# A hybrid convolution and attention layer on one core: the causal zero block kept in its tiles, sixteen modulation dots beside the attention heads, gate products in twos, and a paired last quarter

## The chip, the cores and the metric

The kernel runs on one core of one Trainium2 chip. The metric is the device time of one execution in microseconds (us), the median of several runs. Each engine (PE, the matrix engine; DVE, the vector engine; ACT, the scalar engine; POOL; SP, which here only issues transfers) takes its own list of instructions in a fixed order, and semaphores hold an instruction back until what it needs is there.

## What is computed

One layer: a modulation vector from the condition `c`, then a mixing sub-layer that runs a causal convolution and stick-breaking attention on the same modulated input and merges them by two gates, and then a SwiGLU sub-layer. Width 1024, 1024 rows, 8 heads of 64, 31 taps, all in float32. Cut to what matters:

```python
mod = silu(c) @ ada_w + ada_b                        # 6 x 1024
sh1, sc1, ga1, sh2, sc2, ga2 = split(mod, 6)
h = rmsnorm(x, pre_mix_g) * (1 + sc1) + sh1
proj = h @ w_in                                      # glu_in, qkv, gates
u = u_val * sigmoid(u_gate)
y_conv = silu(layernorm(causal_depthwise_conv(u))) @ w_conv_out
# stick-breaking attention, causal is strict: s_idx < t_idx
log_keep = where(causal, log_sigmoid(-z), 0)
a = where(causal, exp(log_sigmoid(z) + cumsum_reverse(log_keep) - log_keep), 0)
y_att = (a @ v) @ w_att_out
y = (sigmoid(g_conv) * y_conv + sigmoid(g_att) * y_att) @ w_o
x = x + ga1 * rmsnorm(y, post_mix_g)
h = rmsnorm(x, pre_ffn_g) * (1 + sc2) + sh2
x = x + ga2 * rmsnorm((silu(gate) * up) @ w_ffn_out, post_ffn_g)
```

## The kernel before

Every float32 operand is split into a high and a low part (`hi` and `lo`), and a product is three matmuls; ACT makes the high part and DVE the low one. The stages stand one after the other on PE: norms and first projections to about 70 us; the attention stage from 70 to about 430 us; the early gate products to 500; the rest of the gate products (`other_five`) with the layer norm (`ln_all`) to 560; `y_conv`, `y_att` and the output projection to 760; the SwiGLU products to about 1185; its output sweeps to 1403, and the finish of the last quarter of the output.

In the attention stage `attend(p)` treats head pair p. A head takes blocks of 256 query rows, c = 0 to 3. For each it makes the logits `z` (PE, L551 to L554), two sigmoids (`ka` and `be`, ACT), a scan of products and a multiply (DVE, L559 and L561), and then for each pair of key blocks `jp` four 128 x 128 transposes into one PSUM tile `tr` (PE, L571), a copy to `ahi` (ACT, L574), a subtraction to `alo` (DVE, L575) and four `av` matmuls with the values `vst` (L580, L581). In the diagonal pair (jp == c) one of the four blocks lies behind the causal bound, and a tile `zeros` is transposed for it. Between the heads' instructions stand the gated units `glu(ct)` (products `pgg` and `pgv`, result `u`, stored to `v_d`), `conv(ct)` (`pcv` matmuls, results `co` stored to `u_d`), the value products `v_half` (`pv`, split into `vst` at L485 and L486) and the next pair's `pq` and `pk`. A scheduler of the language sets the order on each engine from the order of the code, from priorities and from its own estimates.

`load` issues a transfer on SP's queue and `store` on POOL's; a queue takes its instructions in order, and one that waits holds up those behind it. A tile with a `tag` and `bufs=1` shares one buffer with all tiles of that tag: the next user waits until the last one is done.

`dot_c` is one column of the modulation vector: a multiply by the condition and a sum along the row on DVE (L135, 128 x 1024). Columns 16 to 31 (`ada2_16` to `ada2_31`), first needed after the output projection, stand between the `y_conv` tiles, two behind each, loaded on SP into two buffers. The last quarter of the output is finished by `finish(..., last=...)`: a root (L151 to L155), two multiplies with it (L1637, L1640) and the add of the residual (`add`, L1540).

## Time and profile before

| | us |
|---|---|
| median of 3 runs (1415.29 to 1421.37) | 1417.07 |
| the profiled execution | 1416.81 |
| span of the profiled execution | 1415.0 |
| PE busy in the span | 1383.6 (98%) |
| DVE busy | 1060.4 (75%) |
| ACT busy | 651.3 (46%) |

The profile is of one execution; its span is the time between the first and the last instruction that it records, and the rest of the device time lies around it. An engine is busy while one of its instructions runs. Matmuls overlap, so that the duration of a single one is longer than the distance to the next. Names are those of the program without buffer numbers, and L12 is line 12 of the kernel.

### The profile page before, as it was taken

To read this page: it belongs to the slowest core of one execution; us is meant where nothing else is said; L and a number is where in the kernel's file an instruction comes from. 1 tells how busy PE (TensorE), PEld (TensorE's weight loads), DVE (VectorE), ACT (ScalarE), POOL (GpSimd) and SP (SyncE) were. 2 spreads that over 40 slices of the span, in tenths; PEclk is the share of its full clock that TensorE was granted. 3 is DMA by queue.
4 is the path that set the end of the run, shared out by engine and by line. 5 is a ranking of instruction groups with operands and counts; after the bars stand their busy time and mean duration, and the time that the engine had idled before them with its cause. 6 is when DMAs were issued, how large, how long until landed. Compare 5 with 4: busy or idle time off the path is not lost.

```text
span 1415.0 us, 18809 instructions
## 1 busy us (share of the span) xinstructions
PE 1383.6 (98%) x6886; PEld 1156.1 (82%) x6886; DVE 1060.4 (75%) x1602; ACT 651.3 (46%) x1136; POOL 96.7 (7%) x183
## 2 busy tenths in 40 slices
PE   7999999999999999999999999999999999999996
PEld 4798898898888878888877778888888887888886
DVE  6898598576767789779588878778877775775357
ACT  5375465364553447412356553334444453334441
POOL 0000000000001110000012100001111110000000
PEclk8999999999999999999999999999999999999998
DMA  9112041131253645784935545456777769588833
GB/s 382 74 37 75 30 141 54 45 114 66 77 177 111 228 179 175 280 277 137 361 120 173 185 147 173 157 173 228 242 255 246 259 245 392 170 333 280 281 116 119
DMA packets 91116, 258.73 MB, mean 183 GB/s; under 512 B 9744, under 2 KB 20112, under 8 KB 90000
## 3 DMA queue, kind: packets, MB, share of 16 engines
q1 hardware_dynamic: 75088, 202.99, 42.1%
q0 software_dynamic: 15936, 54.54, 10.3%
q8 instruction: 54, 0.88, 0.3%
q14 instruction: 38, 0.31, 0.1%
HBM read 190.91 MB, written 66.58 MB: 182 GB/s over the span
## 4 chain that ended last, share of the span: by engine, by line
PE 80%; DVE 6%; issue 6%; DMA 5%; ACT 2%; POOL 1%; SPq 0%; DVEq 0%; POOLq 0%; ACTq 0%
PE ka L958 12%; PE ka L1500 8%; PE kc L958 7%; PE pwo L881 6%; PE pb L1500 4%; PE pgv L180 3%; PE pg L180 3%; PE pyc L180 3%; PE pya L180 3%; PE pv L481 3%; PE pcv L461 3%; PE tr L571 2%; PE pq L180 2%; PE pgg L180 2%; PE pk L180 2%
## 5 line engine op out<-in xcount | busy, mean ns | idle before, releaser
L559 DVE TENSOR_TENSOR_SCAN ka<-ka 128x128 f32<-128x128 f32 (+2 forms) x96 | 91.4, 968 | 22.8 <-ACT ka L555 22.5
L555 ACT ACTIVATE ka<-z 128x128 f32<-128x128 f32 (+2 forms) x96 | 47.1, 496 | 58.8 <-PE z L554 34.4
L575 DVE TENSOR_TENSOR alo<-tr,ahi 128x512 fp32r<-128x512 f32 x80 | 53.2, 685 | 18.2 <-ACT ahi L574 17.5
L1500 PE MATMUL ka<-gt,w2f 128*128 128x512 f32 x264 | 63.4, 390 | 0.8 <-DMA w2f<-w_d 0.8
L574 ACT ACTIVATE ahi<-tr 128x512 fp32r<-128x512 f32 x80 | 46.3, 601 | 38.1 <-PE tr L571 25.8
L561 DVE TENSOR_TENSOR be<-be,ka 128x127 f32<-128x127 f32 (+2 forms) x96 | 53.4, 573 | 9.6 <-ACT be L556 4.9
L1500 PEld LDWEIGHTS ka<-gt,w2f 128*128 128x128 f32 x264 | 49.4, 188 | 11.5 <-issue 1.4
L1066 PE MATMUL ke<-b,w_hi 128*128 128x512 f32 x176 | 55.2, 394 | 0.0
L135 DVE SCALAR_TENSOR_TENSOR ada<-ada,cb 128x1024 f32<-128x1024 f32 x32 | 38.8, 1223 | 20.7 <-DMA ada<-in_ada_dram 20.6
L556 ACT ACTIVATE be<-z 128x128 f32<-128x128 f32 (+2 forms) x96 | 46.2, 495 | 9.5 <-PE tr L571 9.3
L571 PE MATMUL tr<-ident,be 128*128 128x128 f32 x288 | 47.8, 273 | 0.4 <-DVE alo L575 0.4
L580 PE MATMUL av<-ahi,vst 128*128 128x256 f32 x160 | 44.2, 292 | 0.0
L461 PE MATMUL pcv<-ph,cvw 128*128 128x128 f32 x320 | 42.5, 276 | 0.8 <-DMA ph<-v_d 0.8
L581 PE MATMUL av<-alo,vst 128*128 128x256 f32 x160 | 42.8, 293 | 0.0
L461 PEld LDWEIGHTS pcv<-ph,cvw 128*128 128x128 f32 x320 | 39.5, 192 | 1.5 <-issue 1.2
L1066 PEld LDWEIGHTS ke<-b,w_hi 128*128 128x128 f32 x176 | 33.0, 188 | 7.8 <-issue 1.0
L481 PE MATMUL pv<-wv_hi,hhi 128*128 128x256 f32 x128 | 36.8, 288 | 2.1 <-DVE qst L505 1.4
L159 ACT ACTIVATE gt<-X 128x512 fp32r<-128x512 f32 x33 | 20.4, 630 | 39.5 <-DVE X L1543 12.4
L481 PE MATMUL pv<-wv_hi,hlo 128*128 128x256 f32 x128 | 36.7, 287 | 0.0
L481 PE MATMUL pv<-wv_lo,hhi 128*128 128x256 f32 x128 | 36.4, 285 | 0.0
L551 PE MATMUL z<-kst,qst 128*128 128x256 f32 (+2 forms) x96 | 36.2, 382 | 0.0
L571 PEld LDWEIGHTS tr<-ident,be 128*128 128x128 f32 x288 | 34.7, 140 | 1.8 <-PE z L554 0.5
(533 smaller groups left out, 4097.7 us busy)
## 6 DMA issues: line engine op xcount, KB each, us to landing
w_d<-w2o POOLq DMA_DIRECT2D x44, 512.0 KB, 8.0
w2f<-w_d SPq DMA_DIRECT2D x44, 512.0 KB, 5.4
ada<-in_ada_dram SPq DMA_DIRECT2D x32, 512.0 KB, 6.1
w2r<-in_w_dram SPq DMA_DIRECT2D x44, 256.0 KB, 3.8
w1g<-in_w_dram SPq DMA_DIRECT2D x21, 512.0 KB, 3.6
w1u<-in_w_dram SPq DMA_DIRECT2D x21, 512.0 KB, 5.2
cvw<-in_cvw_dram SPq DMA_DIRECT2D x20, 512.0 KB, 3.7
ada_w<-in_ada_dram SPq DMA_DIRECT2D x8, 1024.0 KB, 12.0
```

The source lines that it names most:

```text
L180: pe.matmul(bank, st[:, cols], mv[k][:, c * CH:(c + 1) * CH], start=(i == 0 and s == 0), stop=(i == n - 1 and s == 2))
L461: pe.matmul(cv[:, gi * TM:(gi + 1) * TM], wts[n][:, at:at + P], ph[:, g, SH - 1 - d:SH - 1 - d + TM], start=(d == 0), stop=(d == SH - 1))
L481: pe.matmul(pv[:, :256], st[k][:, tcols], mv[:, wc], start=(k == 0 and i == 0), stop=(k == KT - 1 and i == 2))
L555: act.activation(kap[:, s_lo:s_hi], z[:, zo:zo + w], AF.Sigmoid, bias=0.0, scale=-0.125)
L559: dve.tensor_tensor_scan(rev, rev, rev, init, op0=ALU.mult, op1=ALU.bypass)
L561: dve.tensor_tensor(beta[:, :m], beta[:, :m], kap[:, s_lo + 1:s_lo + 1 + m], op=ALU.mult)
L571: pe.transpose(tr[:, o:o + P], src, ident)
L575: dve.tensor_tensor(alo, tr, ahi, op=ALU.subtract)
L881: pe.matmul(bank_, st[:, cols], mv[k][:, cs], start=(k == 0 and q == 0), stop=(k == KT - 1 and q == 2))
L958: pe.matmul(bank_, st[:, cols], t[:, mv], start=(first and j == 0 and s == 0), stop=(j == HK - 1 and s == 2), skip_group_check=not first)
L1066: pe.matmul(kbs[f], wes[f][st][:, cols], t[:, mv], start=(i == 0 and j == 0 and q == 0), stop=(j == HK - 1 and q == 2), skip_group_check=i ...
L1500: pe.matmul(dst, w[st][:, cols], g[mv], start=first and s == 0, stop=last and s == 2, skip_group_check=more)
```

## The change

Seven edits. (1) The transposes of `zeros` are gone. The diagonal pair goes to one of two lasting pairs of tiles, `diag_t`, whose first 128 columns are set to zero once; the two key blocks of that pair change places in the tile, and the copy and the subtraction cover 384 columns instead of 512. (2) The sixteen dots move from `y_conv` into the attention stage: six behind `glu(0)`, five behind `glu(1)`, five behind `glu(2)`. They are loaded on POOL's queue into the one buffer of tag `u`, which `glu` also uses. The small operations behind the dots (`add_bias`, `fold_gate`) move with them in the order on DVE. (3) The stores of `co` move from SP's to POOL's queue. (4) `conv(3)` moves behind the first plain gate. (5) The early gate products run two gates at a time, and the second product of each is added in the bank of the first: six adds on DVE (L628) are gone. (6) The last tile of `y_att` is finished in two halves with a higher priority, and the rotation of banks is shifted by one. (7) The last quarter's finish copies three residual pieces into PSUM on ACT, does the first of four output pieces on POOL, and adds in 512 columns instead of 256 on DVE.

```diff
@@ conv
-                    load(u_d[ct][hf * (NG // 2):(hf + 1) * (NG // 2)].rearrange("g p m -> p g m"), o)
+                    store(u_d[ct][hf * (NG // 2):(hf + 1) * (NG // 2)].rearrange("g p m -> p g m"), o)
@@ head
+            diag_t = []
+            for i in range(2):
+                t = [pa.tile([P, CH], F32R, name=f"{nm}d{i}") for nm in ("ahi", "alo")]
+                for x in t:
+                    dve.tensor_copy(x[:, :P], zeros)
+                diag_t.append(t)
+            ndiag = count()
...
+                            on = jp == c
                             for jj in range(2):
                                 j = 2 * jp + jj
                                 for ii in range(2):
+                                    if on and jj == 1 and ii == 0:
+                                        continue
                                     jo = (j - 4 * sc) * P
-                                    src = zeros if (jp == c and jj == 1 and ii == 0) else probs[ii][:, jo:jo + P]
-                                    o = jj * 256 + ii * P
-                                    pe.transpose(tr[:, o:o + P], src, ident)
-                            ahi = pa.tile([P, CH], F32R, tag="ahi", name=f"ahi{tag}_{c}_{jp}", bufs=2)
-                            alo = pa.tile([P, CH], F32R, tag="alo", name=f"alo{tag}_{c}_{jp}", bufs=2)
-                            act.activation(ahi, tr, AF.Copy)
-                            dve.tensor_tensor(alo, tr, ahi, op=ALU.subtract)
+                                    o = (jj ^ on) * 256 + ii * P
+                                    pe.transpose(tr[:, o:o + P], probs[ii][:, jo:jo + P], ident)
+                            if on:
+                                ahi, alo = diag_t[next(ndiag) % 2]
+                                used = slice(P, CH)
+                            else:
+                                ahi = pa.tile([P, CH], F32R, tag="ahi", name=f"ahi{tag}_{c}_{jp}", bufs=2)
+                                alo = pa.tile([P, CH], F32R, tag="alo", name=f"alo{tag}_{c}_{jp}", bufs=2)
+                                used = slice(0, CH)
+                            act.activation(ahi[:, used], tr[:, used], AF.Copy)
+                            dve.tensor_tensor(alo[:, used], tr[:, used], ahi[:, used], op=ALU.subtract)
...
-                                cols = slice(jj * 256, jj * 256 + 256)
+                                cols = slice((jj ^ on) * 256, (jj ^ on) * 256 + 256)
@@ the attention stage
+            a2 = deque(range(2 * KT, 4 * KT))
+
+            def ada2_dots(n):
+                for _ in range(n):
+                    col = a2.popleft()
+                    w = pc.tile([P, D], F32, tag="u", name=f"ada2_{col}", bufs=1)
+                    store(w, ada2[col - 2 * KT])
+                    dot_c(w, cb, col)
+
             for p in range(4):
                 glu(p)
+                ada2_dots((6, 5, 5, 0)[p])
                 if p == 2:
                     v = v_half(1)
                 if p:
                     conv(p - 1)
                 qk = attend(p, qk, v)
-            conv(3)
             for n in PLAIN:
+                if n == PLAIN[1]:
+                    conv(3)
...
-            for i in GPAIRS:
...
-                k2 = bank(f"k2_{i}")
-                prod0(k2, w_op(f"a12_{i}", raw[:, CH:], act, dve), "B21")
-                dve.tensor_tensor(e[1], k2, e[0], op=ALU.add)
-                act.activation(e[1], e[1], AF.Sigmoid, bias=0.0, scale=1.0)
+            for i0 in range(0, len(GPAIRS), 2):
+                two = GPAIRS[i0:i0 + 2]
...
+                for i in two:
+                    prod0(ek[i], a12[i], "B21", False)
+                    e1 = sgp.tile([P, CH], F32, tag="sg", name=f"ee1_{i}", bufs=2)
+                    act.activation(e1, ek[i], AF.Sigmoid, bias=0.0, scale=1.0)
+                    store(s_d[2 * i][:, :CH], e1)
@@ y_conv and y_att
-            ada2_dots(y_conv(n), 2)
+            y_conv(n)
...
+        next(uidg)
...
+            if n == KT - 1:
+                hi, lo = (hp.tile([P, T], F32R, tag="act", name=f"{nm}{n}") for nm in ("mhi", "mlo"))
+                for c in range(NCH):
+                    gemm({c: yb[c]}, wa, (ohi, olo), range(4), woff=(n % 2) * CH)
+                with tc.high_priority(offset=LASTM):
...
@@ finish
+            if last:
+                xp = {}
+                for mm_ in (2, 3, 1):
+                    xp[mm_] = bank(f"x1p{mm_}").rearrange("p (a b) -> p a b", a=2)
+                    act.activation(xp[mm_], xrs[c, mm_][:, :, cols], AF.Copy)
             rstd_from(rs, m, a, ps_sum, D)
+            if last:
...
+                pool.tensor_tensor(y0, y0, r2, op=ALU.mult)
+                pool.tensor_tensor(y0, y0, xrs[c, 0][:, :, cols], op=ALU.add)
+                for m, y in ((2, y2_), (3, y3)):
+                    for i in range(2):
+                        dve.scalar_tensor_tensor(y[:, i], last[2 * (m - 2) + i][:, cols],
+                                                 gpost2[:, 2 * m + i:2 * m + i + 1], rs, op0=ALU.mult, op1=ALU.mult)
+                    add(dve, y, y, xp[m])
+                    put(m, y)
+                dve.tensor_tensor(y1, y1, r2, op=ALU.mult)
+                add(dve, y1, y1, xp[1])
+                put(0, y0)
+                put(1, y1)
+                pin(begin)
+                return
```

How the instructions stand. On PE, at one diagonal pair of a head (`tr1_0_2_2` is pair p 1, head 0, block c 2, key pair 2), before and then in the change:

```order
L571 MATMUL tr1_0_2_2_1827<-ident_135,be1_0_4_1_1808 128x128
L571 MATMUL tr1_0_2_2_1827<-ident_135,be1_0_5_1_1818 128x128
L571 MATMUL tr1_0_2_2_1827<-ident_135,zeros_147 128x128
L571 MATMUL tr1_0_2_2_1827<-ident_135,be1_0_5_1_1818 128x128
L551 MATMUL z1_0_6_1_1884<-kst1_0_1147,qst1_0_1145 128x384
```
```order
L597 MATMUL av1_0_0_1741<-alod1_579,vst0_2_679 128x256
L582 MATMUL tr1_0_2_2_1838<-ident_135,be1_0_4_1_1819 128x128
L582 MATMUL tr1_0_2_2_1838<-ident_135,be1_0_5_1_1829 128x128 x2
L181 MATMUL pgv1_1_1606<-hhi1_281,wgv1_hi_1601 128x512
L181 MATMUL pgv1_1_1606<-hlo1_282,wgv1_hi_1601 128x512
```

The transpose of `zeros` is gone, and what stands behind the three others has changed; over the program PE has 32 instructions fewer.

On DVE, around the last two splits of the second half of the values (`vst1_6<-pv1_7` is the last of them; the `av` products of head pair 2 need it), before and then in the change, where `ada2_31` is the last of the sixteen dots:

```order
L559 SCALAR_TENSOR_TENSOR ka2_1_0_3174<-ka2_1_0_3174 128x128
L559 SCALAR_TENSOR_TENSOR ka2_1_1_3184<-ka2_1_1_3184 128x256
L486 TENSOR_TENSOR vst1_6_2660<-pv1_6_2661,vst1_6_2660 128x4x64
L561 TENSOR_TENSOR be2_1_0_0_3175<-be2_1_0_0_3175,ka2_1_0_3174 128x127
L561 TENSOR_TENSOR be2_1_1_0_3185<-be2_1_1_0_3185,ka2_1_1_3184 128x255
L575 TENSOR_TENSOR alo2_0_3_2_2980<-tr2_0_3_2_2974,ahi2_0_3_2_2979 128x512
L486 TENSOR_TENSOR vst1_6_2660<-pv1_7_2688,vst1_6_2660 128x4x64
```
```order
L487 TENSOR_TENSOR vst1_6_2668<-pv1_6_2669,vst1_6_2668 128x4x64
L136 SCALAR_TENSOR_TENSOR ada2_31_2488,mod_156<-ada2_31_2488,cb_176 128x1024
L570 TENSOR_TENSOR be2_1_2_0_3201<-be2_1_2_0_3201,ka2_1_2_3200 128x383
L142 TENSOR_TENSOR mod_156<-mod_156,vec_133 128x16
L570 TENSOR_TENSOR be2_1_3_0_3211<-be2_1_3_0_3211,ka2_1_3_3210 128x511
L149 TENSOR_TENSOR gpost1_159<-mod_156,vec_133 128x8
L1017 TENSOR_TENSOR dsh_6401<-mod_156 128x4
L591 TENSOR_TENSOR alod0_575<-tr2_1_0_0_3190,ahid0_574 128x384
L487 TENSOR_TENSOR vst1_6_2668<-pv1_7_2696,vst1_6_2668 128x4x64
```

The last split now stands behind the last dot and six smaller operations.

On DVE, the end of the program (the last quarter's finish; `frs01` is the root, `x1p` a residual piece in PSUM), before and then in the change:

```order
L155 SCALAR_TENSOR_TENSOR frs01_12178<-frs01a_12180,frs01_12178 128x256
L1637 TENSOR_TENSOR yc11_0_11976<-yc11_0_11976,frs01_12178 128x256 x2
L1637 TENSOR_TENSOR yc11_1_11977<-yc11_1_11977,frs01_12178 128x256 x2
L1640 SCALAR_TENSOR_TENSOR yc21_0_11984<-ka_0_10335,gpost2_160,frs01_12178 128x256
L1640 SCALAR_TENSOR_TENSOR yc21_0_11984<-ka_1_10336,gpost2_160,frs01_12178 128x256
L1640 SCALAR_TENSOR_TENSOR yc21_1_11985<-ka_2_10337,gpost2_160,frs01_12178 128x256
L1640 SCALAR_TENSOR_TENSOR yc21_1_11985<-ka_3_10338,gpost2_160,frs01_12178 128x256
L1540 TENSOR_TENSOR yc11_0_11976<-yc11_0_11976,xr0_0_11964 128x256 x2
L1540 TENSOR_TENSOR yc11_1_11977<-yc11_1_11977,xr0_1_11967 128x256 x2
L1540 TENSOR_TENSOR yc21_0_11984<-yc21_0_11984,xr0_2_11970 128x256 x2
L1540 TENSOR_TENSOR yc21_1_11985<-yc21_1_11985,xr0_3_11973 128x256 x2
```
```order
L156 SCALAR_TENSOR_TENSOR frs01_12080<-frs01a_12082,frs01_12080 128x256
L1683 SCALAR_TENSOR_TENSOR yc21_0_11886<-ka_0_10237,gpost2_160,frs01_12080 128x256
L1683 SCALAR_TENSOR_TENSOR yc21_0_11886<-ka_1_10238,gpost2_160,frs01_12080 128x256
L1575 TENSOR_TENSOR yc21_0_11886<-yc21_0_11886,x1p2_12083 128x2x256
L1683 SCALAR_TENSOR_TENSOR yc21_1_11887<-ka_2_10239,gpost2_160,frs01_12080 128x256
L1683 SCALAR_TENSOR_TENSOR yc21_1_11887<-ka_3_10240,gpost2_160,frs01_12080 128x256
L1575 TENSOR_TENSOR yc21_1_11887<-yc21_1_11887,x1p3_12085 128x2x256
L1687 TENSOR_TENSOR yc11_1_11879<-yc11_1_11879,frs01_12080 128x2x256
L1575 TENSOR_TENSOR yc11_1_11879<-yc11_1_11879,x1p1_12087 128x2x256
```

Sixteen operations behind the root have become eight, and the first piece (`yc11_0`) has left DVE for POOL.

## Rows read from the trace of the kernel before

**Rows 1.** The profile's page: busy time of PE and DVE in the span, their busy tenths in forty slices with PE's granted clock, and the chain that ended last by engine.
```profile
PE 1383.6 (98%) x6886; PEld 1156.1 (82%) x6886; DVE 1060.4 (75%) x1602; ACT 651.3 (46%) x1136; POOL 96.7 (7%) x183
PE   7999999999999999999999999999999999999996
...
DVE  6898598576767789779588878778877775775357
...
PEclk8999999999999999999999999999999999999998
...
PE 80%; DVE 6%; issue 6%; DMA 5%; ACT 2%; POOL 1%; SPq 0%; DVEq 0%; POOLq 0%; ACTq 0%
```

**Rows 2.** Busy time by stage: the stretch, its length, and then the busy us (and instructions) of PE, PE's weight loads, DVE, ACT and POOL, the granted clock, the transfers' share and GB/s.
```profile
120.00:200.00 80.00, 80.00 (x470) 68.78 (x469) 60.84 (x84) 43.02 (x88) 0.00 (x0) 1.00 0.19 61
200.00:300.00 100.00, 100.00 (x646) 89.07 (x646) 68.87 (x99) 50.33 (x103) 5.64 (x3) 1.00 0.20 64
300.00:400.00 100.00, 98.87 (x636) 87.36 (x635) 75.64 (x107) 58.09 (x122) 0.25 (x2) 1.00 0.34 111
400.00:500.00 100.00, 99.85 (x495) 84.05 (x495) 66.56 (x96) 43.52 (x84) 10.39 (x19) 1.00 0.55 181
500.00:560.00 60.00, 57.81 (x243) 44.90 (x243) 57.08 (x93) 37.90 (x57) 6.50 (x12) 1.00 0.43 145
...
600.00:640.00 40.00, 40.00 (x178) 33.15 (x177) 32.37 (x49) 6.26 (x6) 0.00 (x0) 1.00 0.82 277
...
1380.00:1415.00 35.00, 23.83 (x184) 22.95 (x182) 26.12 (x57) 6.46 (x18) 0.00 (x0) 0.88 0.34 121
```

**Rows 3.** What PE waited for: its instruction, what released it, us in total, times, longest.
```profile
PE ka L415 <- DVE gv L703: 1.2, 1, 1.2
...
PE kc L415 <- DVE gw L705: 0.8, 1, 0.8
PE pcv L461 <- DMA ph<-v_d: 0.8, 1, 0.8
...
PE tr L571 <- DVE alo L575: 0.4, 1, 0.4
```

**Rows 4.** The transposes of `zeros`: count, shortest, median and longest in ns, first and last start.
```profile
L571 PE MATMUL tr<-ident,zeros x32: 270/273/279, 84.9 to 417.6; 128*128 128x128 f32 x32
```

**Rows 5.** PE in order of time around one transpose of `zeros`: start, us, instruction.
```profile
192.30 0.28 PE L571 MATMUL tr<-ident,zeros 128*128 128x128 f32 x1
192.41 0.60 PE L571 MATMUL tr<-ident,be 128*128 128x128 f32 x4
192.77 0.36 PE L551 MATMUL z<-kst,qst 128*128 128x256 f32 x1
```

**Rows 6.** The dots and their loads over the whole program (32 of them, half of which move): ns shortest, median and longest; and how long the loads took from issue to landing.
```profile
L135 DVE SCALAR_TENSOR_TENSOR ada<-ada,cb x32: 1215/1224/1228, 591.2 to 1279.0; 128x1024 f32<-128x1024 f32 x32
L135 DVE DVE_READ_ACCUMULATOR ada<-ada,cb x32: 80/83/85, 592.3 to 1280.1; 128x1 f32 x32
...
DMA to landing us min/median/max: 3.6/6.1/9.8
```

**Rows 7.** Transfers issued between 60 and 460 us: queue, count, KB each, median us from issue to landing.
```profile
cvw<-in_cvw_dram SPq DMA_DIRECT2D x20, 512.0 KB, 3.7
...
v_d<-u SPq DMA_DIRECT2D x4, 512.0 KB, 2.9
...
u_d<-co SPq DMA_DIRECT2D x8, 256.0 KB, 3.8
...
s_d<-sg POOLq DMA_DIRECT2D x8, 256.0 KB, 2.9
wq_raw<-in_win_dram SPq DMA_DIRECT2D x3, 512.0 KB, 3.6
```

**Rows 8.** In order of time, on DVE the third gated unit `u`, and on PE the beginning of the second half of the value products.
```profile
266.91 2.02 DVE L443 TENSOR_TENSOR u<-pgv,sg 128x512 f32<-128x512 f32 x2 [0.54 <-PE pgv L180]
...
266.94 0.28 PE L481 MATMUL pv<-wv_hi,hhi 128*128 128x256 f32 x1
267.05 0.28 PE L481 MATMUL pv<-wv_hi,hlo 128*128 128x256 f32 x1
```

**Rows 9.** The end of the program on DVE in order of time, with a run of four 512-column operations on DVE and one 1024-column operation on POOL from earlier.
```profile
1405.37 0.42 DVE L155 SCALAR_TENSOR_TENSOR frs<-frs01a,frs 128x256 f32<-128x256 f32 x1
1405.83 1.43 DVE L1637 TENSOR_TENSOR yc<-yc,frs 128x256 f32<-128x256 f32 x4
1407.18 1.65 DVE L1640 SCALAR_TENSOR_TENSOR yc<-ka,gpost,frs 128x256 f32<-128x256 f32 x4
1408.75 2.76 DVE L1540 TENSOR_TENSOR yc<-yc,xr 128x256 f32<-128x256 f32 x8
...
506.95 2.49 DVE L741 TENSOR_TENSOR cr<-cr,lm 128x512 f32<-128x512 f32 x4
...
254.61 3.03 POOL L169 TENSOR_TENSOR wv_lo<-wv_raw,wv_hi 128x1024 fp32r<-128x1024 f32 x1 [13.89 <-ACT wv_hi L159]
```

**Rows 10.** What DVE waited for between 440 and 560 us: us in total, times, longest.
```profile
DVE ee L628 <- DMA s_d<-ee: 6.5, 3, 4.4
...
DVE gs L695 <- DMA gw3b<-in_win_dram: 1.2, 1, 1.2
```

More of the change, by code (lines that the diff above doesn't have):

```diff
@@ L46 @@
 LN_PRI = 100
+LASTM = 200
 LN_DVE0 = (0, 1)
@@ L617, in tile_block @@
                     store(s_d[n][:, c * CH:(c + 1) * CH], sg)
-            for i in GPAIRS:
-                raw = wp.tile([P, T], F32, tag="wraw", name=f"ew{i}")
-                load(raw, win[20 + 2 * i])
-                e = [sgp.tile([P, CH], F32, tag="sg", name=f"ee{q}_{i}", bufs=2) for q in range(2)]
-                k1 = bank(f"k1_{i}")
-                prod0(k1, w_op(f"a11_{i}", raw[:, :CH], act, dve), "B11")
-                act.activation(e[0], k1, AF.Copy)
-                store(e_d0[i], e[0])
-                k2 = bank(f"k2_{i}")
-                prod0(k2, w_op(f"a12_{i}", raw[:, CH:], act, dve), "B21")
-                dve.tensor_tensor(e[1], k2, e[0], op=ALU.add)
-                act.activation(e[1], e[1], AF.Sigmoid, bias=0.0, scale=1.0)
-                store(s_d[2 * i][:, :CH], e[1])
+            for i0 in range(0, len(GPAIRS), 2):
+                two = GPAIRS[i0:i0 + 2]
+                ek, a12 = {}, {}
+                for i in two:
+                    raw = wp.tile([P, T], F32, tag="wraw", name=f"ew{i}")
+                    load(raw, win[20 + 2 * i])
+                    ek[i] = bank(f"k1_{i}")
+                    prod0(ek[i], w_op(f"a11_{i}", raw[:, :CH], act, dve), "B11")
+                    a12[i] = w_op(f"a12_{i}", raw[:, CH:], act, dve)
+                    e0 = sgp.tile([P, CH], F32, tag="sg", name=f"ee0_{i}", bufs=2)
+                    act.activation(e0, ek[i], AF.Copy)
+                    store(e_d0[i], e0)
+                for i in two:
+                    prod0(ek[i], a12[i], "B21", False)
+                    e1 = sgp.tile([P, CH], F32, tag="sg", name=f"ee1_{i}", bufs=2)
+                    act.activation(e1, ek[i], AF.Sigmoid, bias=0.0, scale=1.0)
+                    store(s_d[2 * i][:, :CH], e1)
     sV.close()
@@ L762, in ln_all @@
                 cacc[ct] = o
-        a2 = deque(range(2 * KT, 4 * KT))
-        def ada2_dots(ins, n):
-            for _ in range(n):
-                col = a2.popleft()
-                w = pg.tile([P, D], F32, tag="f", name=f"ada2_{col}", bufs=2)
-                load(w, ada2[col - 2 * KT])
-                with tc.issue_after(ins.ins):
-                    dot_c(w, cb, col)
         def y_conv(n):
@@ L782, in y_conv @@
                 cs = slice(c * CH, (c + 1) * CH)
-                last = dve.tensor_tensor(y[:, cs], yb[c], y[:, cs], op=ALU.mult)
+                dve.tensor_tensor(y[:, cs], yb[c], y[:, cs], op=ALU.mult)
             yc.append(y)
-            return last
         pair_load(GPAIRS[0])
@@ L815, in tile_block @@
             yb = {c: bkg(f"pya{n}_{c}") for c in range(NCH)}
+            y = yc[n]
+            if n == KT - 1:
[3 more added lines that the diff above has]
+                with tc.high_priority(offset=LASTM):
+                    for c in range(NCH):
+                        cs = slice(c * CH, (c + 1) * CH)
+                        load(sg[c], s_d[8 + n][:, cs])
+                        last = dve.tensor_tensor(sg[c], yb[c], sg[c], op=ALU.mult)
+                        dve.tensor_tensor(y[:, cs], y[:, cs], sg[c], op=ALU.add)
+                        act.activation(hi[:, cs], y[:, cs], AF.Copy)
+                        dve.tensor_tensor(lo[:, cs], y[:, cs], hi[:, cs], op=ALU.subtract)
+                mhi.append(hi)
+                mlo.append(lo)
+                break
             gemm(yb, wa, (ohi, olo), range(4), woff=(n % 2) * CH)
-            y = yc[n]
             for c in range(NCH):
@@ L825, in tile_block @@
             mlo.append(lo)
-        assert not a2
         add_bias(16, 32)
```

5 lines of the change are left out of this document (added).

## The prediction

> **What bounds the kernel now.** I read the page first. PE is busy for 1383.6 of the 1415.0 us, at its upper clock level nearly everywhere, and 80% of the chain that ended last lies on it [rows 1]. So an edit pays in two ways only: it takes instructions from PE, or it closes one of the few gaps that PE has. The table by stage says where those gaps are. From 120 to 300 us, from 400 to 500 and from 600 to 640 PE is busy for the whole of each stretch but 0.15 us; 300 to 400 lacks 1.13 us, 500 to 560 lacks 2.2, and the last 35 us lack 11.2, the tail in which PE has nothing left [rows 2]. In the same stretches DVE is busy for 61 of 80, 69 of 100 and 76 of 100 us: it has room in the heads, but not at every moment, since its order is fixed [rows 2]. PE's own list of waits names the gaps: 0.8 us for the load of `ph` and 0.4 for an `alo`, both near 392 us, and 1.2 and 0.8 us for the gate products, between 500 and 515 [rows 3].
>
> **The zero block.** 32 transposes of `zeros` leave PE. Each has a duration of 0.273 us [rows 4], which would make 8.7 us. But matmuls overlap. What counts is the distance from one start to the next: 192.30 to 192.41, then four more transposes in 0.60 us, of which the last takes some 0.27, so (0.60 - 0.27) / 3 = 0.11 [rows 5]. 32 times 0.11 is **3.5 us**, and since PE stands full there [rows 2], the path gets all of it unless DVE or ACT becomes late. Bounds: 0 and 8.7. DVE and ACT gain too, a quarter of 32 subtractions and copies, and two more pairs of tiles are in rotation; neither engine is the bound, so I count nothing.
>
> The Trainium skill, "TensorE: Matmul & The Clock Gate", Part 4 (PE-mode transpose), gives about 275 ns for a 128 x 128 transpose in a kernel's context, with access latency the larger part. The row's 273 ns agrees as a duration; as a price per transpose the distance of 0.11 us contradicts it. By that page the term would be 8.8 us instead of 3.5, an estimate, and the time 1406.7.
>
> **The dots leave `y_conv`.** There PE is full: 40.00 of 40 us around them [rows 2]. Taking 8 x 2 x 1.3 = 21 us of work from DVE (1.22 + 0.08 each, [rows 6]) brings nothing there.
>
> **The dots in the heads.** They cost DVE the same 21 us, within 100 us or so of idle time. The danger is their order. All sixteen pass through one buffer, which the gated unit's `u` uses as well: a load can be issued only when the dot before is done, and DVE, when it comes to a dot whose load has not landed, stands still with all behind it. A round is a load and a dot. The trace has no 512 KB load on POOL's queue. Near it: 512 KB on SP's queue in this stage 3.6 to 3.7 us; 256 KB on POOL's 2.9 against 3.8 on SP's [rows 7]; the dots' own loads, in other stages, 3.6 at the least and 6.1 in the median [rows 6]. I take 3.7, the rows of the same stage and size, and keep 6.1 as the upper end. A round is then 3.7 + 1.3 + 0.1 for the signals (a guess) = 5.1 us.
>
> The tightest place is the third run, dots 27 to 31. I set the clock to the start of the value products, 266.94 us [rows 8]. `u` is done at +2.0 (266.91 + 2.02), its store lands 2.9 later [rows 7], and five rounds of 5.1 end at +30.4. Then come seven shorter operations up to the last split of the values, at about 0.34 each (four 256-column ones in 1.43 us, [rows 9]): +32.8. PE needs that split in the second half of an `av` product. By the changed order it has until then 226 matmuls of 256 columns at 0.12 [rows 8] = 27.1, 35 of 128 columns at 0.11 = 3.9, and 14 logits and masks for about 2: **33.0 us**. So the two are level, and each tenth on a round costs 0.5 us. The first run (six dots) has, counted in the same way, some 0.6 us to spare per round, and the second more, because its first two dots stand later in the order. I take 1 us for the third run and 0.5 for the others: **+1.5 us**, 0 at the best; the upper end is a rival below. Behind a waiting dot are queued scans, `alo` and `vst`; PE and, through them, the next heads wait for these.
>
> **The stores of `co` on POOL's queue.** They stand behind loads of dots and now and then delay one; `u_d` is first read by the layer norm, behind the early gates. Nothing.
>
> **`conv(3)` later.** The 0.8 us wait for `ph` is gone if other work of PE stands there; the 0.4 us for `alo` may go with it or not [rows 3]. I take **-0.8** (0 to -1.2).
>
> **Early gates in twos.** DVE loses six adds and the 6.5 us wait for stores before them [rows 10]. PE stands at 99.85 of 100 us there [rows 2], so there is nothing to win; the next pair's first copy now waits for the second pair's store, with PE's other bank as cover. Nothing, +1 without that cover. The same holds for the last `y_att` tile, behind which PE has no wait now.
>
> **Gate products and layer norm, 500 to 560 us.** Here DVE is nearly full (57 of 60) and PE waits for it, 2.0 us in two waits [rows 2, 3]. An add and a wait for a weight load (1.2 us, [rows 10]; two loads of dots no longer stand on SP's queue near it) are gone. What is late next is the following operation of DVE, so I take a third: **-0.7** (+1 to -2).
>
> **The tail.** Behind the root DVE works from 1405.83 to 1408.75 + 2.76 = 1411.51: 5.7 us [rows 9]. After: four multiplies as before, 1.65; four operations of 512 columns at 0.60 ((2.49 - 0.69) / 3, [rows 9]), 2.4; and three places where an operation needs the one just before (0.1 each, 1405.37 to 1405.83 against 0.34), 0.3. That is 4.35, so **-1.3**. POOL's two operations: 1024 columns took 3.03 us [rows 9], 512 then 1.5, twice that 3.0: within the 4.35. If POOL takes twice as long, the gain is gone.
>
> The Trainium skill, "SBUF — State Buffer", section "SBUF: two separate sides", says that a DVE operation with two inputs in SBUF and a POOL operation that reads SBUF exclude each other for a whole instruction. Only the multiply of the second piece on DVE is of that kind beside POOL. No row of before shows such a pair; if it held here at the worst moment, one POOL operation would eat the tail's gain, and the sum would end at 1413.3, an estimate.
>
> **Sum.** -3.5 + 1.5 - 0.8 - 0.7 - 1.3 = -4.8. Against the profiled execution's 1416.81 that is **1412.0 us**; the median of the runs shown is 1417.07, 0.26 higher. Half a per cent of it is 7.1 us, about what a measurement of this kernel can tell from no change: faster means under 1410.0, slower over 1424.2.
>
> **Rivals.**
> *Slower, by the loads.* If the loads take 6.1 us as the dots' loads did in the median [rows 6], each round is 2.4 longer: the third run loses 5 x 2.4 = 12, the first 5 x (2.4 - 0.6) = 9, the second perhaps 4, together 25 instead of 1.5: 1435.5. It decides from 5.4 us per load (5 x 1.7 + 5 x 1.1 = 14, so 1424). Against it: the transfers are lightly used in the heads (61 to 111 GB/s between 120 and 400 us against 277 in `y_conv`, [rows 2]), and every 512 KB load on SP there took 3.6 to 3.7 [rows 7]. Chance 0.11.
> *No gain.* The heads are bound by turns by PE and by chains through ACT and DVE, and what leaves PE comes back as waits for `alo` or `be`, with 21 us more on DVE. Then -3.5 and -0.8 fall away: 1416.3. For it: the 0.4 us wait for `alo` [rows 3] shows that DVE can be last. Against it: 0.4 us is all in 300 us. Chance 0.18.
> *Faster.* A transpose is worth its 0.273 us, or the stretch 500 to 560 closes its 2.2 us [rows 2] and the tail and the dots go at their best: -3.5 + 0 - 1.2 - 2 - 1.6 = -8.3; by the first, -10. So 1406.8 to 1408.5. Chance 0.29.
> *The forecast*, 1410 to 1415: 0.42.
>
> **Range.** The fast case sets the lower end at 1405 (some 0.06 lie below), the no-gain case with a longer round 1421 above (0.13 lie over it, the slow case above all). Faster by over 0.5% 0.29; within it 0.42 + 0.18 = 0.60; slower 0.11. The likeliest case by itself holds 1410 to 1415.
>
> **What would show it.** Right: PE 3 to 4 us less busy by the start of the early gates, no wait of PE for `vst` or `alo` over 1 us, loads of the dots landing at 3.5 to 4 us, the wait for `ph` gone, and some 4.4 us of DVE behind the last root. Wrong: dots' loads over 4.5 us with `av` or `pv` waiting behind them; or a stage earlier by 8 us at the end of the heads, so that the transposes were worth their duration; or new waits in the pairs of early gates.

## The result and the profile after

The changed kernel took 1420.47 us (median of 20 runs, 1417.22 to 1424.93), the kernel before 1415.14 in the runs beside it: a ratio of 1.0037, interval 1.0026 to 1.0047. It is slower by some 5 us, 0.37%. That is within 0.5%, where the prediction put 0.60, and inside its range, but on the other side of no change than its 1412.0. The profiled execution took 1424.08 us, and its span is 6.9 us longer than the one before; 3.8 of these lie in its start, where PE's granted clock was 0.50 of full (the lower of its two levels, 1.2 GHz) from 28 to 40 us against a mean of 0.73 before, in work that the change leaves alone, while a second profile of the same kernel (`change_again` below) starts like the one before.

The page after (busy time; PE's clock; the chain that ended last), beside [rows 1]:

```profile
PE 1387.6 (98%) x6854; PEld 1157.7 (81%) x6854; DVE 1050.3 (74%) x1593; ACT 651.8 (46%) x1140; POOL 112.9 (8%) x209
...
PEclk8899999999999999999999999999999999999998
...
PE 78%; DVE 6%; issue 6%; DMA 5%; ACT 2%; POOL 1%; SPq 0%; DVEq 0%; POOLq 0%; ACTq 0%
```

PE has 32 instructions fewer and the chain is nearly as before, so the page doesn't tell where the time went. The stages do. The same table as [rows 2], of the second profile:

```profile
120.00:200.00 80.00, 78.79 (x452) 66.66 (x450) 65.48 (x94) 40.87 (x85) 3.89 (x7) 1.00 0.29 94
200.00:300.00 100.00, 97.44 (x605) 83.97 (x604) 73.40 (x111) 48.90 (x100) 11.27 (x14) 1.00 0.34 116
...
400.00:500.00 100.00, 98.58 (x516) 84.00 (x515) 68.22 (x99) 45.99 (x91) 11.80 (x21) 1.00 0.50 170
500.00:560.00 60.00, 58.86 (x251) 46.68 (x250) 56.21 (x88) 39.18 (x57) 5.95 (x11) 1.00 0.42 136
```

PE had no gap from 120 to 300 us before; now 3.8 us are missing there, and 1.4 between 400 and 500. Its waits in the heads, still from the second profile (70 to 446 us; instruction, releaser, us in total, times, longest), beside [rows 3]:

```profile
PE pg L181 <- ACT wg_hi L160: 1.4, 1, 1.4
PE av L597 <- DVE alo L591: 1.3, 1, 1.3
PE tr L582 <- DVE be L570: 1.2, 3, 0.8
...
PE tr L582 <- DVE alod L591: 0.6, 2, 0.4
PE av L596 <- DVE vst L487: 0.5, 1, 0.5
```

The wait for `ph` is gone, and five others are there: 5.0 us instead of 1.2 (two more, left out, are the same in both). To set the stages beside each other I use three landmarks on PE: the first value product `pv`, the first early gate product `k`, and the first product of the output projection `pwo`. A row gives count, shortest, median and longest in ns, then first and last start. Before, and then the second profile:

```profile
L481 PE MATMUL pv<-wv_hi,hhi x128: 274/283/384, 70.0 to 295.6; 128*128 128x256 f32 x128
L415 PE MATMUL k<-hhi,a x96: 389/389/389, 457.0 to 492.1; 128*128 128x512 f32 x96
L881 PE MATMUL pwo<-mhi,wo_hi x88: 389/389/798, 665.9 to 725.9; 128*128 128x512 f32 x88
```
```profile
L482 PE MATMUL pv<-wv_hi,hhi x128: 274/283/384, 70.3 to 302.2; 128*128 128x256 f32 x128
L416 PE MATMUL k<-hhi,a x96: 389/389/390, 461.4 to 498.5; 128*128 128x512 f32 x96
L916 PE MATMUL pwo<-mhi,wo_hi x88: 389/389/798, 669.4 to 729.4; 128*128 128x512 f32 x88
```

From `pv` to `k` (the heads) it was 457.0 - 70.0 = 387.0 us and is 391.1: **+4.1** (+2.2 in the first profile, 389.2). From `k` to `pwo` 208.9 and 208.0: -0.9 (-0.8 in the first). So the heads lost where they were to gain 2.8. PE has the same matmuls between the landmarks in both kernels, but for the 32 transposes. Its waits between `pv` and `k` sum to 1.8 us before and 5.7 now (4.4 in the first profile); without them the stretch took 385.2 us before and 385.4 now (384.8), so the 32 transposes that are gone show no gain there either.

The end of the first profile of the change, beside [rows 9] (DVE and POOL in order of time; below them the DRAIN instructions that close POOL's and SP's queue: count, shortest, median and longest ns, first and last start):

```profile
1409.36 0.42 DVE L156 SCALAR_TENSOR_TENSOR frs<-frs01a,frs 128x256 f32<-128x256 f32 x1
1409.82 0.88 DVE L1683 SCALAR_TENSOR_TENSOR yc<-ka,gpost,frs 128x256 f32<-128x256 f32 x2
1410.01 1.26 POOL L1679 TENSOR_TENSOR yc<-yc,frs 128x512 f32<-128x512 f32 x1 [219.06 <-DVE frs L156]
...
1411.35 1.26 POOL L1680 TENSOR_TENSOR yc<-yc,xr 128x512 f32<-128x512 f32 x1
...
1413.56 0.69 DVE L1575 TENSOR_TENSOR yc<-yc,x1p 128x512 f32<-128x512 f32 x1
...
L1848 POOLq DRAIN  x3: 40/93/9807, 1411.3 to 1421.6; - x3
...
L1848 SPq DRAIN  x3: 7/7/7, 1416.7 to 1421.4; - x3
```

DVE works for 4.43 us behind the root (1409.82 to 1414.25), where it took 5.68 before. SP, which waits for the last stores, is through at 1416.7. But POOL's closing DRAIN begins beside its last operation, at 1411.3, and lasts 9.81 us, to 1421.1. Nothing else runs for the last 4.4 us. Before, POOL's long drain lay at 1186 us, behind the issue of its last transfer, beside other work:

```profile
L1786 POOLq DRAIN  x3: 40/93/8429, 1185.9 to 1414.8; - x3
```

The stretch from `pwo` to the root got 1.2 us shorter (before 1405.4 - 665.9 = 739.5; after 1409.4 - 671.1 = 738.3). PE's work there is the same, and two runs that leave it as it was have 737.8 (`tail_alone`, 665.2 to 1403.0) and 737.2 (`small_pool_op`, 666.6 to 1403.8): the profiled execution of before took longer there than they do. So this isn't a gain of the change.

### The profile page after: what moved, and what is told of

Read it like the earlier page. It is cut to its first block, busy times and chain, and to the rows that moved or that the text cites. A ratio compares the mean times of both kernels' runs of the same rounds, so it can differ in the third digit from the quotient of the medians.

```text
span 1421.9 us, 18704 instructions
## 1 busy us (share of the span) xinstructions
PE 1387.6 (98%) x6854; PEld 1157.7 (81%) x6854; DVE 1050.3 (74%) x1593; ACT 651.8 (46%) x1140; POOL 112.9 (8%) x209
## 3 DMA queue, kind: packets, MB, share of 16 engines
q0 software_dynamic: 18880, 65.02, 12.5%
## 4 chain that ended last, share of the span: by engine, by line
PE 78%; DVE 6%; issue 6%; DMA 5%; ACT 2%; POOL 1%; SPq 0%; DVEq 0%; POOLq 0%; ACTq 0%
PE ka L993 14%; PE ka L1535 8%; PE kc L993 8%; PE pwo L916 6%; PE pb L1535 4%; PE pg L181 3%; PE pyc L181 3%; PE pya L181 3%; PE pgv L181 3%; DMA ada<-in_ada_dram 3%; PE k L416 2%; PE pa L1535 2%; PE ka L416 2%; PE kb L993 2%; PE pcv L462 2%
## 5 line engine op out<-in xcount | busy, mean ns | idle before, releaser
L590 ACT ACTIVATE ahi<-tr 128x512 fp32r<-128x512 f32 x48 | 28.1, 601 | 23.2 <-PE tr L582 19.1
L591 DVE TENSOR_TENSOR alo<-tr,ahi 128x512 fp32r<-128x512 f32 x48 | 32.0, 682 | 7.0 <-ACT ahi L590 6.8
L160 ACT ACTIVATE s1o<-s 128x512 fp32r<-128x512 f32 x22 | 13.8, 629 | 49.7 <-PE ka L993 42.3
L1101 PE MATMUL ke<-b,w_lo 128*128 128x512 f32 x88 | 34.6, 394 | 1.4 <-DVE w_lo L1035 1.4
```

What stands on the lines that cost most here:

```text
L1101: pe.matmul(kbs[f], wes[f][st][:, cols], t[:, mv], start=(i == 0 and j == 0 and q == 0), stop=(j == HK - 1 and q == 2), skip_group_check=i ...
```

## Experiments

Fourteen runs; `change_again` is the change itself, the others put parts of it back or take parts of it alone. "Before" in a ratio is the kernel before, run beside it on the same chip (medians 1415.1 to 1415.8). The expectations count from the medians known when they were written. The last column is from one profile per run: kernels with the same code in the heads agree to 0.2 us there, the change itself only to 1.9 (389.2, 390.6 and 391.1 in three profiles).

| run | median us | ratio (interval) | `pv` to `k`, us |
|---|---|---|---|
| the change | 1420.47 | 1.0037 (1.0026 to 1.0047) | 389.2 |
| `change_again` | 1421.40 | 1.0042 (1.0027 to 1.0057) | 391.1 |
| `after_y0_on_dve` | 1417.69 | 1.0016 (1.0005 to 1.0027) | 390.6 |
| `tail_alone` | 1414.76 | 0.9990 (0.9981 to 1.0000) | 387.1 |
| `zero_block_alone` | 1420.35 | 1.0034 (1.0021 to 1.0047) | 385.3 |
| `dots_alone` | 1422.59 | 1.0056 (1.0038 to 1.0074) | 392.1 |
| `dots_back` | 1417.85 | 1.0017 (1.0006 to 1.0027) | 384.6 |
| `dots_own_loads` | 1417.56 | 1.0015 (1.0003 to 1.0026) | 387.7 |
| `small_pool_op` | 1415.14 | 0.9999 (0.9990 to 1.0007) | 387.1 |
| `dots_back_y0_on_dve` | 1417.55 | 1.0012 (1.0001 to 1.0023) | 384.8 |
| `co_stores_on_sp` | 1415.04 | 1.0006 (0.9996 to 1.0017) | 386.2 |
| `small_pool_op_co_stores` | 1413.43 | 0.9996 (0.9983 to 1.0008) | 386.9 |
| `no_dots_no_queue` | 1416.40 | 0.9999 (0.9985 to 1.0012) | 385.1 |
| `own_loads_co_on_sp` | 1414.55 | 0.9993 (0.9981 to 1.0005) | 386.9 |
| `zero_block_and_dots` | 1414.99 | 1.0002 (0.9989 to 1.0016) | 385.7 |

**The tail: POOL's share taken out, and the tail alone.**

```diff
# after_y0_on_dve, against the change
-                pool.tensor_tensor(y0, y0, r2, op=ALU.mult)
-                pool.tensor_tensor(y0, y0, xrs[c, 0][:, :, cols], op=ALU.add)
...
+                dve.tensor_tensor(y0, y0, r2, op=ALU.mult)
+                add(dve, y0, y0, xrs[c, 0][:, :, cols])
+                put(0, y0)
...
-                put(0, y0)
# tail_alone, against before: the `if last:` blocks of finish alone
```

> The changed kernel with the first output piece of the last quarter done on DVE instead of POOL (two operations of 512 columns more on DVE, about 1.2 us). In the trace of the change POOL's closing drain lasts from 1411.3 to 1421.1 us, 4.4 us longer than anything else. Theory A, that drain behind POOL's last arithmetic sets the end: it is gone, the time falls by 4.4 - 1.2 = 3.2 us against the change, to about +2 us over the kernel before. Rival B, the end is set by DVE and the last stores and the drain only fills idle time: the time rises by 1.2 us. Rival C, POOL's operations themselves are late and their piece is stored late: falls by under 1 us.

> The kernel before with the paired last quarter alone, POOL's share as in the change. By theory A: DVE's part ends 1.3 us earlier, but the end comes with POOL's drain, so +2.5 to +3.5 us (1418) against the kernel before. By the prediction as it stood: -1.3 us (1413.5).

With the piece on DVE the kernel is 2.8 us faster (theory A said 3.2): the drain did set the end. But the tail alone cost nothing, against theory A as it stood: its median is 1.0 us under the kernel before, with an interval that reaches no change. Its trace has the same two POOL operations and the same idle time of 218 us before them, and yet a shorter drain:

```profile
1404.95 1.27 POOL L1645 TENSOR_TENSOR yc<-yc,xr 128x512 f32<-128x512 f32 x1
...
L1813 POOLq DRAIN  x3: 40/93/6131, 1404.9 to 1411.6; - x3
L1813 SPq DRAIN  x3: 7/7/7, 1410.3 to 1411.3; - x3
```

Behind the end of the last operation (1406.2) it lasts 4.8 us, where the change has 8.5 (1412.6 to 1421.1). So what had the change done to POOL's drain?

**What the drain's length follows.**

```diff
# small_pool_op, against before
+            if last:
+                tiny = sq_tile("tiny")[:, :1]
+                pool.tensor_tensor(tiny, rs[:, :1], rs[:, :1], op=ALU.mult)
# small_pool_op_co_stores: the same and
-                    load(u_d[ct][hf * (NG // 2):(hf + 1) * (NG // 2)].rearrange("g p m -> p g m"), o)
+                    store(u_d[ct][hf * (NG // 2):(hf + 1) * (NG // 2)].rearrange("g p m -> p g m"), o)
# co_stores_on_sp, against the change
-                    store(u_d[ct][hf * (NG // 2):(hf + 1) * (NG // 2)].rearrange("g p m -> p g m"), o)
+                    load(u_d[ct][hf * (NG // 2):(hf + 1) * (NG // 2)].rearrange("g p m -> p g m"), o)
```

> The kernel before with one added POOL operation on a single column behind the last root, whose result nobody reads. Theory A (POOL's closing drain is long whenever POOL has worked shortly before): the drain begins at the root and lasts 6 to 10 us; from the root to the span's end there are 9.2 us in the kernel before, so the time rises by 0 to 2 us. Rival J (the drain is long because the two 512-column operations really run that long): drain under 2 us, no change.

> The kernel before with the small POOL operation behind the last root and, beside it, the eight stores of co moved to POOL's queue; nothing else. Theory K: drain of 7.2 us behind the operation instead of 4.83, which then ends at about the span's end (0 to +1 us). Rival L: 4.83 again.

> The changed kernel with the eight stores of co back on SP's queue, all else as in the change. In the runs so far POOL's closing drain, counted from the end of its last operation, is 4.83 us in two kernels with the 164 POOL transfers of the kernel before, 7.20 in two with the eight stores added, 8.51 in the change with the sixteen loads added as well. Theory K, the drain's length follows what POOL's queue has issued: 4.83 + 1.31 = 6.1 us here, and the time 2.4 us under the change. Rival L, it follows the place or the idle time before: 8.5 again, time as the change.

POOL's long drain in `small_pool_op`, `small_pool_op_co_stores`, `dots_back`, `dots_own_loads`, `co_stores_on_sp`, `own_loads_co_on_sp` and `change_again`, in this order:

```profile
L1789 POOLq DRAIN  x3: 40/93/5196, 1404.4 to 1413.2; - x3
...
L1789 POOLq DRAIN  x3: 40/93/7567, 1402.2 to 1411.1; - x3
...
L1849 POOLq DRAIN  x3: 40/102/8502, 1408.8 to 1417.9; - x3
...
L1848 POOLq DRAIN  x3: 40/93/8501, 1410.1 to 1419.2; - x3
...
L1848 POOLq DRAIN  x3: 40/102/7441, 1404.7 to 1412.7; - x3
...
L1848 POOLq DRAIN  x3: 40/102/6131, 1405.2 to 1411.8; - x3
...
L1848 POOLq DRAIN  x3: 40/93/9808, 1408.6 to 1418.9; - x3
```

The drain begins with the last operation, which takes 0.33 us in the first two and 1.27 in the others. Counted from that operation's end:

| POOL's queue issues, in the whole program | drain behind the last operation, us |
|---|---|
| what it issues before (`tail_alone`, `small_pool_op`, `own_loads_co_on_sp`, `no_dots_no_queue`) | 4.8, 4.8, 4.8, 4.8 |
| that and the 16 loads of dots (`co_stores_on_sp`) | 6.1 |
| that and the 8 stores of `co` (`dots_back`, `dots_own_loads`, `small_pool_op_co_stores`) | 7.2, 7.2, 7.2 |
| that and both (the change, `change_again`) | 8.5, 8.5 |

Theory K holds to a tenth in ten profiles, with one operation of a single column as with two large ones, and whatever lies around. The transfers that POOL issued hundreds of microseconds ago make its closing drain longer: 8 stores by 2.4 us, 16 loads by 1.3. The other six profiles bear it out at another size. There POOL's last instruction is the issue of a transfer near 1190 us, and the drain ends behind the landing of that transfer by 2.4 us in two kernels with the transfers of before (before, `zero_block_alone`), 3.1 in two with the loads of dots more (`dots_alone`, `zero_block_and_dots`), 3.6 with the stores more (`dots_back_y0_on_dve`) and 4.3 with both (`after_y0_on_dve`): half of 4.8, 6.1, 7.2 and 8.5. Why half, no run shows.

A store of `co` has rows of 512 bytes, but on POOL's queue it isn't more packets than a load. The pages count (packets, MB, share) before, with the 8 stores more (`dots_back`), and with the 16 loads more (`co_stores_on_sp`):

```profile
q0 software_dynamic: 15936, 54.54, 10.3%
...
q0 software_dynamic: 16576, 56.63, 10.7%
...
q0 software_dynamic: 18240, 62.93, 12.1%
```

That is 80 packets for a store and 144 for a load: the loads bring more packets and more bytes, and lengthen the drain less. Why a store costs more stays open. With the stores back on SP's queue and nothing else undone, the change is 5.4 us faster by the medians (4.4 by the ratios), 1415.04: as fast as the kernel before.

**The heads: each part alone.**

```diff
# zero_block_alone: the edits in head() and diag_t alone
# dots_alone, against before
+                ada2_dots((6, 5, 5, 0)[p])      # in the attention stage, loaded by store() into tag "u"
-            ada2_dots(y_conv(n), 2)
+            y_conv(n)
# zero_block_and_dots: both
```

> The kernel before with the causal zero block kept in its tiles and nothing else. By the distance of starts (0.11 us each): -3.5 us. By the duration of one (0.273 us): -8.7. By the rival that PE's saving comes back as waits or as more changes between kinds of matmul: -1 to +1.

> The kernel before with the sixteen dots moved beside the heads, loaded on POOL's queue into the one buffer of u, and nothing else. The trace of the change has rounds of 5.5 us (landing 3.9, issue 0.35 behind the dot, dot 1.3) and PE waits of 0.2 to 1.25 us for be, alo and vst behind dots. Theory D, the dots are what the heads lost: +2.5 to +5 us. Rival E, the dots cost 1.5 or less and the heads lost by the changed order of the zero block: 0 to +1.5.

> The kernel before with the zero block kept and the dots in the heads on POOL's queue, co stores on SP's queue, nothing else. If costs add (zero block -1.2 and dots +5.0 at 440 us, each alone): PE +3.8 us at 440 us. If the dots' cost lies in the order that the scheduler makes around them: near the -0.8 that the change showed with the co stores on SP's queue.

The heads get 1.7 us shorter by the zero block, 5.1 longer by the dots, and 1.3 shorter by both: the costs don't add. The scheduler makes another order on all engines in each case. In `dots_alone` PE waits for `alo` three times (1.7 us) and once each for `qst`, `wq_hi` and `vst` (1.1, 0.5, 0.3); with the zero block beside the dots two waits of 0.4 for `alo` are left. Theory D, that the dots are the heads' loss, falls with the pair. Waits are half of it: in `dots_alone` they sum to 2.4 us more than before, and the stretch without them is 2.6 longer, at a granted clock of 1.00 as before. The same products start further apart there; the profile names no cause, and it stays open.

The zero block alone is slower by 4.6 us all the same, and this shows in its trace behind the heads (the wait, then busy time by stretch as in [rows 2]):

```profile
PE pwo L896 <- DVE sga L836: 3.4, 1, 3.4
```
```profile
660.00:670.00 10.00, 6.64 (x26) 5.14 (x25) 8.35 (x12) 3.06 (x3) 0.00 (x0) 0.84 0.31 104
670.00:680.00 10.00, 10.00 (x38) 8.12 (x37) 1.49 (x2) 1.06 (x1) 0.00 (x0) 0.82 0.90 307
680.00:690.00 10.00, 10.00 (x45) 8.28 (x45) 4.86 (x5) 6.26 (x9) 0.00 (x0) 1.00 1.04 402
...
668.00:670.00 2.00, 1.93 (x5) 1.57 (x6) 2.00 (x3) 0.00 (x0) 0.00 (x0) 0.50 0.63 256
670.00:672.00 2.00, 2.00 (x6) 1.56 (x5) 0.88 (x2) 1.06 (x1) 0.00 (x0) 0.50 0.76 256
```

The output projection waits 3.4 us for the last tiles of `y_att`, which are late on DVE, and the granted clock (the column before the transfers' share) falls from 1.00, the upper level (2.4 GHz), to a mean of 0.84 and 0.82: 38 matmuls instead of 45 in the second ten microseconds. In steps of two microseconds it is at the lower level, 0.50, from 668 to 672 us, and back at 1.00 from 674. From the first to the last start of `pwo` it takes 62.7 us instead of 60.0. A wait of 3.4 us cost 6.1. In the change there is no such wait: the dots are gone from that stretch and the merge is finished in halves. With the dots put back there, it is 1.2 (`dots_back`) and 1.7 (`no_dots_no_queue`); with the dots away and the old merge 1.7 (`zero_block_and_dots`), and 1.7 in `dots_alone`. Behind these four shorter waits the clock stayed at 1.00, and `pwo` took 60.1 to 60.2 us.

**The dots put elsewhere.**

```diff
# dots_back: the dots between the y_conv tiles as before; all else as in the change
# dots_back_y0_on_dve: also the first output piece on DVE
# dots_own_loads, against the change
-                    w = pc.tile([P, D], F32, tag="u", name=f"ada2_{col}", bufs=1)
-                    store(w, ada2[col - 2 * KT])
+                    w = wp.tile([P, D], F32, tag="wraw", name=f"ada2_{col}")
+                    load(w, ada2[col - 2 * KT])
```

> The changed kernel with the sixteen dots back between the y_conv tiles, loaded on SP's queue into two buffers; all else as in the change, POOL's share of the tail too. Theory D (the dots in the heads cost 4 to 5 us there, as in the run of the dots alone): the time falls by 3 to 5 us against the change, to 1415 to 1417. Rival E (they cost 1.5): falls by 1 to 1.5. Rival F: their 21 us on DVE beside y_conv delay the merge, PE waits at the output projection and its clock falls, as in the run of the zero block alone: no fall, or a rise of 2 to 4.

> The changed kernel with both suspects out: the dots back between the y_conv tiles, and the first output piece on DVE. By theories A and D together: -2.5 and -3 to -5 against the change, 1412 to 1414, so 1 to 3 us under the kernel before. If the dots' place is not the cause: 1417, as with the piece on DVE alone.

> The changed kernel with the dots in the same stage, but loaded on SP's queue into the several buffers of the weights, so that a load need not wait for the dot before. Theory G, the single buffer's round of 5.5 us is what costs: waits of PE behind dots go, -2 to -4 us against the change. Rival H, DVE's 1.3 us per dot at that place is what costs: within 1 us of the change. Rival I: the weights' loads are now late instead: slower than the change by 1 to 4.

Without the dots the heads are 4.6 to 6.5 us shorter than in the change's two profiles (384.6), and the kernel 2.6 us faster; a part of the rest is the wait at the merge. `dots_back_y0_on_dve` missed its 1412 to 1414: its profile ends 9.4 us behind the root instead of the 11.2 of `dots_back`, but its median is only 0.3 us lower: without both suspects the kernel comes near the kernel before (1.0012, from 1.0001) and not under it. With own loads on SP's queue the heads take 387.7 and the kernel is 2.9 us faster. Neither reaches the kernel before, since both keep the `co` stores on POOL's queue and so a drain of 7.2.

**What is left of the change.**

```diff
# no_dots_no_queue: the change with dots, co stores and conv(3) as before
# own_loads_co_on_sp: dots_own_loads and the co stores on SP's queue
# change_again: the change itself
```

> What the runs leave of the change: the zero block kept, early gates in twos, the merge's last tile in halves and the paired last quarter with POOL; the dots are back between the y_conv tiles, the co stores on SP's queue and conv(3) in its old place. Heads about 2 us under the kernel before, drain 4.83 and so the tail -0.8, a wait at the merge of 0 to 3: 1412 to 1415, that is -3 to 0 us against the kernel before.

> The changed kernel with the dots loaded on SP's queue into the buffers of the weights and the co stores on SP's queue: POOL's queue as in the kernel before. Theory K: drain 4.83 again. Theory M, the co stores on POOL's queue cost the heads 2 to 3 us through the dots' loads behind them: with neither there, heads -1 us against before and the time 1412.5 to 1414, under both kernels. If the heads' loss is only a matter of which order the scheduler makes: any value from 1412 to 1418.

> The changed kernel once more, for a profile with an early rise of the clock at the start, beside which the stages can be set directly. Theory: heads +2 us at 440 us against the kernel before, drain 8.51 behind POOL's last operation, span 4 to 5 us longer. Rival: the heads' loss in the first profile belonged to the late rise of the clock, and PE is level or ahead at 440 us.

Neither of the first two is clear of the kernel before: the better, 1414.55, has an interval up to 1.0005. `change_again` bears out that the heads' loss has nothing to do with the late clock.

**What the stores do in the heads.** `change_again` and `co_stores_on_sp` differ in that one word, and the heads in 391.1 against 386.2. The trace of the first around dot 24, on POOL's queue, DVE and PE:

```profile
208.57 0.53 POOL L108 DMA_DIRECT2D ada<-in_ada_dram  x1 [5.87 <-DVE ada L136]
...
211.71 0.77 POOL L108 DMA_DIRECT2D u_d<-co  x1 [2.48 <-ACT co L466]
...
216.42 1.23 DVE L136 SCALAR_TENSOR_TENSOR ada<-ada,cb 128x1024 f32<-128x1024 f32 x1 [1.79 <-DMA ada<-in_ada_dram]
...
224.34 0.69 DVE L591 TENSOR_TENSOR alo<-tr,ahi 128x512 fp32r<-128x512 f32 x1
...
225.09 0.38 PE L597 MATMUL av<-alo,vst 128*128 128x256 f32 x1 [1.28 <-DVE alo L591]
```

The dot's load was issued at 208.57 and landed 7.8 us later; a store of `co` was issued 3.1 us behind it, on the same queue. DVE stood for 1.79 us at the dot, nothing between there and `alo` has a gap to spare, and PE waits 1.28 us. With the stores on SP's queue the scheduler places the same dot four operations later, its load lands in 6.3 us, and DVE doesn't wait. That dot is not alone. What DVE waited for the dots' loads between 60 and 450 us, with the stores on POOL's queue and on SP's (us in total, times, longest):

```profile
DVE ada L136 <- DMA ada<-in_ada_dram: 21.8, 12, 3.5
...
DVE ada L136 <- DMA ada<-in_ada_dram: 15.8, 13, 2.9
```

So the wait is shown; how much of the 4.9 us is the queue and how much the other order that the scheduler made for it, no run parts. But without dots' loads on POOL's queue the stores cost the heads little or nothing. `small_pool_op_co_stores` has them on POOL's queue without dots there, with PE's order nearly that of before, and its heads take 386.9 us against 387.0 and 387.1 (`small_pool_op`); `dots_back`, with the stores on that queue and the dots behind the heads, has 384.6 against 385.1 in `no_dots_no_queue`; and `dots_own_loads`, with the dots' loads on SP's queue, has 387.7 against 386.9 in `own_loads_co_on_sp`.

## Why the prediction was wrong, step by step

- **The zero block, -3.5.** By the distance of starts, not by the duration, is right: nothing shows 8.7, and the heads gained 1.7 alone, 1.9 and 2.4 with the other edits but without the dots (385.1 and 384.6). Alone, the stretch without waits got 2.8 shorter, near the term, and 1.1 came back as waits (for `ph` 1.6 instead of 0.8, for `be` 0.6, the 0.4 for `alo` gone). This was the rival "no gain", half true. In the change nothing of the gain is left. The Trainium skill, "TensorE: Matmul & The Clock Gate", Part 4, states a duration of some 275 ns, and the duration here agrees (270 to 279 ns, [rows 4]). Read as a price per transpose, which the page doesn't say, it would have been 8.8 us (an estimate), and at most 2.8 came.
- **The dots, +1.5.** The single load was well sized: median 3.9 us against 3.7, and a round of 5.5 instead of 5.1, as the load is issued 0.4 behind the dot. With the `co` stores on SP's queue the dots cost 0.4 us (385.7 against 385.3) or 1.1 (386.2 against 385.1). The term held, but only in those orders (the second pair differs in the place of `conv(3)` as well); by themselves they cost 5.1. That a sum of parts holds at all was the silent assumption that failed. The slack was placed wrongly too: the second run of dots was to have the most to spare and the third the least, but PE's waits were 0.9 and 1.2 us beside the first run (the two profiles of the change), 1.3 and 1.7 beside the second, 0.4 and 0.7 beside the third.
- **The `co` stores on POOL's queue, nothing.** This is the step that failed. I looked at who reads `u_d`, not at what the stores do beside the dots' loads and at the end: with them the heads lose 3.0 and 4.9 us in two profiles, and the drain grows by 2.4. Undone alone, 5.4 us of the loss are gone (4.4 by the ratios). By what path the heads lose stays open, since the order changes with the queue: of the loss, the drain's part is shown to its mechanism, the heads' part only to the edit.
- **`conv(3)`, -0.8.** The wait for `ph` is gone as forecast; the second plain gate now waits for its weights instead (`pg` for `wg_hi`, 1.2 and 1.4 us): nothing won. With `conv(3)` in its old place the wait for `ph` was there again (1.5 us, `no_dots_no_queue`).
- **Gates in twos, 0; gate products and norm, -0.7.** No wait of PE in the pairs; from `k` to `pwo` -0.8 and -0.9. The number fits, but three kernels that leave the stretch alone lie between 207.0 and 209.5 us there (208.2 in `tail_alone`), so no gain is shown.
- **The tail, -1.3.** DVE's part is right: 4.35 forecast, 4.43 measured. POOL's operations took 1.26 us each, under the 1.5 I had. The step that failed is "POOL within DVE's 4.35": it counted POOL's operations and not what POOL does behind them. The end moved by +2.9 behind the root (1421.9 - 1409.4 = 12.5 against 9.6). With the drain of 4.8 (`tail_alone`) the end was 8.8 us behind the root, 0.8 less than before. The rule of the Trainium skill, "SBUF — State Buffer", "SBUF: two separate sides", was not put to the test: POOL had ended 0.2 us before the one DVE multiply of that kind began.
- **The merge, 0.** Right for the change, but for a reason I didn't see: alone, the zero block runs into a wait of 3.4 us there.

The slower rival was named for another cause (loads of 6.1 us in the median): the median was 3.9, and behind the longest load, 7.4 and 7.8 in the two profiles, beside a store, PE waited 1.25 and 1.28 us. The sum was off by 10 (-4.8 forecast, counted from an execution of 1416.81; +5.3 measured, from the median of 1415.14): heads 5 to 7, tail 4.2. Of its signs of being right, the loads, the wait for `ph` and DVE's 4.4 us came; a PE less busy by 3 to 4 us and no wait for `alo` over 1 us didn't.

## What to carry to other kernels

Don't put a move of a transfer to another queue at nothing: price it beside everything else that this queue carries, and, for POOL, at the end of the program. The same eight stores cost the heads under 1 us where no dots' loads stood on their queue, and 3 to 5 us where they did. If POOL is to do arithmetic in the last ten microseconds, look for its closing drain in the trace first. And where a scheduler orders the work, parts that were measured one by one don't add up: measure the pair.

## What the runs showed of the hardware

POOL's closing drain took 4.8 us behind its last operation with the transfers that POOL's queue issued before, 6.1 with 16 loads of 512 KB more, 7.2 with 8 stores of 256 KB more, 8.5 with both, and the same to 0.01 us in kernels that differ elsewhere; where POOL has done nothing for 200 us it is over by the end and costs nothing. In six such kernels it ended 2.4 to 4.3 us behind the landing of POOL's last transfer, half of the figure for the same transfers. And a wait of PE of 3.4 us, in a stretch at the upper clock level, went with a fall of the granted clock to 0.50 until about 674 us, nearly six microseconds behind the end of the wait; that cost 2.7 us, nearly as much as the wait itself. Four waits of 1.2 to 1.7 us at the same place left the clock at 1.00.
